# The mixer's input projection as plain fp32 products of the weights as loaded

## The chip, the cores and the metric

The kernel runs on one core of a Trainium2 chip. The time is device microseconds of one launch; three runs of the kernel before took 1105.32, 1108.52 and 1110.19 us (median 1108.52). The profile is one more execution, of 1107.35 us.

## The reference

Two layers work on 256 tokens of width 1024. Each layer is a gated feed-forward net (FFN), a token mixer and a second FFN, and each of these three adds its result to x and normalises:

```
mod = (silu(c) @ ada_w[l] + ada_b[l]).reshape(B, 3, 3, 1, 1024)
h = layernorm(x) * (1 + scale) + shift                     # from mod, for each of the three
f = (silu(h @ w_gate) * (h @ w_up)) @ w_down               # the FFN, inner width 2816
z = h @ w_in                                               # the mixer: 1024 -> 2048
q, k, v, u_ssm, u_pool = split(z, 512, 512, 512, 256, 256)
y = concat(dilated_attention(q, k, v), s5(u_ssm), pooling(u_pool)) @ w_out
x = layernorm(2**0.5 * x + w * gate * result) * gain + bias    # w = 1/2 for an FFN, 1 for the mixer
```

All inputs and outputs are fp32. The change is in `z = h @ w_in`, which is done twice, once in each layer.

## The kernel before

The 256 tokens are two tiles of 128 (called token tile 0 and 1, `tt` in the code). Weights come in pieces of 128 x 1024 fp32 (512 KB), each with one DMA from SyncE (line 374), into 41 slots of SBUF that all large tiles share. A weight piece `raw` is split into two fp32r tiles: ScalarE copies it to `hi` (line 379), VectorE writes `lo = raw - hi` (line 380). The activations are split in the same way into the two halves of `HT` (lines 508 and 509, in `parts`). A product is then three matmuls with one pass each, hi by hi, lo by hi, hi by lo (lines 544 to 546 in `linear`, 556 and 561 in `project`).

The input projection is four groups of 512 columns, named B (the inputs of S5 and pooling), V, Q and K. Each group has four weight pieces and is computed for both token tiles: 8 steps of 128 rows for each, so 64 steps of three matmuls in a layer and 128 in the kernel. Results are `pB`, `pV`, `pQ`, `pK`.

The mixer then runs, for each token tile: transposes (`ptr`), the S5 recurrence (matmul `pbu`, rotations and scans `w` on VectorE and GpSimd, matmul `py`), attention scores (`psc`, added to the bias `lg`, line 975), softmax, transposes of the weights (`ppt`), the weighted sum (`po`), pooling (`pz`), a gate (`pg`) and the output projection (`dm`).

Between two parts stands a chain for each token tile: `y` from the products (line 522), sums and statistics, the new x (line 453), statistics again with a power on GpSimd (line 441), `z` (line 471), a transpose `pn` on TensorE, the modulated `h` on ScalarE (line 481), and its split into `HT`. Two FFN units of token tile 0 can run while token tile 1 is in its chain.

Nobody writes the order by hand. Each operation is recorded with an engine and a cost, and a planner (`Plan.order`) simulates all engines, the slots and the PSUM banks, and emits the operations by planned start. On every engine the emitted order is then fixed: an instruction that waits holds back all behind it.

Of the kernel before, what the change touches and what calls it, by code (L numbers as in the profile page):

```python
# [48 lines left out]
LAG = {"PE": 0.2, "DVE": 0.14, "ACT": 0.14, "Pool": 0.12, "SP": 0.0}  # L49
SAME = {"PE": 0.003, "DVE": 0.125, "ACT": 0.125, "Pool": 0.1, "SP": 0.0}  # L50
WAIT = {"DVE": 0.25, "ACT": 0.25, "Pool": 1.3}
BUFS = {"w": N_W, "th": 2, "a": 2, "aT": 2, "st": 3, "carry": 1, "a3": 1, "gu": 2, "t": 2, "d0": 1, "d1": 1, "d2": 1, "d3": 1}
FREELY = ("t",)
PSUM_KINDS = ("gu", "t", "d0", "d1", "d2", "d3")
# [210 lines left out]
class Build:  # L265
    def __init__(self, tc, io, pools):
        self.tc, self.nc, self.io, self.pools = tc, tc.nc, io, pools
        self.plan = Plan()
        self.items, self.next = [], 0
        self.ready, self.acc, self.bc = {}, {}, {}  # L270
        self.exd, self.turns = [], []


# [94 lines left out]
    def process(self):  # L368

        nc = self.nc  # L370
        x = self.items[self.next]
        self.next += 1
        t = self.slot("raw")
        self.load(lambda: nc.sync.dma_start(out=t[:], in_=self.src(x)), [], [t], 0.5)
        if x[0] == "ada" and x[3] == 0:
            self.start_sum(*x[1:3])
        if x[0] in ("gu", "wd", "win", "wout"):
            hi, lo = self.slot("hi", F32R), self.slot("lo", F32R)
            self.act(1024, lambda: nc.scalar.copy(out=hi[:], in_=t[:]), [t], [hi])  # L379
# [77 lines left out]
    def modulated(self, tt, l, sub):  # L457

        for h, pt in enumerate(self.normed(tt, ("t", "t"))):
            hs = self.slot("h") if h == 0 else hs  # L460
            for k in range(4 * h, 4 * h + 4):
                self.shifted(hs, pt, k, tt, l, sub)
            self.parts(lambda h=h, hs=hs: hs[:, h * 512:(h + 1) * 512].rearrange("p (k t) -> p k t", k=4), [(hs, 4 * h + b) for b in range(4)], 4 * h, 4, tt)
# [20 lines left out]
    def first(self):  # L484

        pts = [list(self.normed(tt, ("t", "t") if tt == 0 else ("d2", "d3"))) for tt in range(2)]
        hs = [self.slot("h") for _ in range(2)]
        for k in range(8):
            for tt in range(2):
                self.shifted(hs[tt], pts[tt][k // 4], k, tt, 0, 0)  # L490
                self.parts(lambda tt=tt, k=k: hs[tt][:, k * 128:(k + 1) * 128].unsqueeze(1), [(hs[tt], k)], k, 1, tt)
# [43 lines left out]
    def linear(self, out, tt, pieces):  # L535

        nc = self.nc
        for kt in range(8):
            hi, lo = self.need(pieces[kt // 2])

            def go(kt=kt, hi=hi, lo=lo):
                xh, xl = (self.HT[:, p, kt, tt * 128:(tt + 1) * 128] for p in range(2))
                c = slice(kt % 2 * 512, kt % 2 * 512 + 512)
                nc.tensor.matmul(out[:], xh, hi[:, c], start=kt == 0, stop=False)  # L544
                nc.tensor.matmul(out[:], xl, hi[:, c], start=False, stop=False)  # L545
                nc.tensor.matmul(out[:], xh, lo[:, c], start=False, stop=kt == 7)  # L546
# [43 lines left out]
    def unit(self, l, sub, f, tt, u, d):  # L590
        nc = self.nc
        ps = self.bank("gu")
        self.linear(ps, tt, [("gu", l, f, u, q) for q in range(4)])
        th = self.buf("th", [128, 256])
        a = self.buf("a", [128, 256])
        self.act(256, lambda: nc.scalar.activation(out=th[:], in_=ps[:, 0:256], func=AF.Silu), [ps], [th])  # L596
        self.dve(256, lambda: nc.vector.tensor_tensor(out=a[:], in0=th[:], in1=ps[:, 256:512], op=ALU.mult), [th, ps], [a])  # L597
        pt = self.bank(shape=(128, 2, 128), name="pa")
        self.pe(0.22, lambda: [nc.tensor.transpose(pt[:, b, :], a[:, b * 128:(b + 1) * 128], self.ident[:]) for b in range(2)], [a, self.ident], [pt])  # L599
        t = self.buf("aT", [128, 2, 2, 128], F32R)  # L600
        self.act(256, lambda: nc.scalar.copy(out=t[:, 0], in_=pt[:]), [pt], [(t, 0)])  # L601
        self.dve(256, lambda: nc.vector.tensor_tensor(out=t[:, 1], in0=pt[:], in1=t[:, 0].bitcast(F32), op=ALU.subtract), [pt, (t, 0)], [(t, 1)])  # L602

        def down():
            for kk in range(2):
                w = self.need(("wd", l, f, u, kk))
                self.project(d, lambda kk=kk: t[:, 0, kk, :], lambda kk=kk: t[:, 1, kk, :], [t], w, u == 0 and kk == 0, u == NU - 1 and kk == 1)
        return down


# [211 lines left out]
    def mixer(self, l):  # L822
# [164 lines left out]
        def attend(tt):  # L987
# [13 lines left out]
            def go():  # L1001
                for h in range(8):
                    for i in range(tt + 1):
# [1 line left out]
            self.pe(1.75 * (tt + 1), go, keys + [(place("v"), ("v", i)) for i in range(tt + 1)], [p])  # L1005
            self.dve(512, lambda: nc.vector.tensor_tensor(out=ya(), in0=p[:], in1=dn[:, 0, tt, :].unsqueeze(2).to_broadcast([128, 8, 64]), op=ALU.mult),
                     [p, (dn, (0, tt))], [(place("qf"), ("f", tt))])
            self.turned(lambda k: qf()[:, tt, k * 128:(k + 1) * 128], [(place("qf"), ("f", tt))], 4, 0, tt)

        def glu(tt):  # L1010

# [15 lines left out]
            for d in range(2):  # L1027
                o = l * 2 + d
                self.act(128, lambda d=d, o=o: nc.scalar.activation(out=z[:, d, :], in_=pg[:, d, :], func=AF.Tanh, scale=0.25, bias=self.hb[:, o:o + 1]),
                         [pg, self.hb], [z], 0.1)  # L1030
            self.dve(256, lambda: nc.vector.scalar_tensor_tensor(out=z[:], in0=z[:], scalar=1.0, in1=yv[:], op0=ALU.add, op1=ALU.mult), [z, yv], [z])
            kh, kl = [[(HT, (p, kt, tt)) for kt in (4, 5)] for p in range(2)]
            self.act(256, lambda: nc.scalar.activation(out=HT[:, 0, 4:6, c], in_=z[:], func=AF.Copy, scale=0.5), [z], kh)
            self.dve(256, lambda: nc.vector.scalar_tensor_tensor(out=HT[:, 1, 4:6, c], in0=z[:], scalar=0.5, in1=HT[:, 0, 4:6, c].bitcast(F32),
# [4 lines left out]
        def pooling(tt):  # L1039
# [27 lines left out]
            self.pe(0.429, lambda: [nc.tensor.matmul(pz[:, j, :], px()[:, j, :], zp[:, j, :], start=True, stop=True) for j in range(2)], [zp, place("pg")], [pz])  # L1067
            c = cols[tt]
            for j in range(2):
                o = O_PS + l * 2 + j  # L1070
                kh, kl = [[(HT, (p, 6 + j, tt))] for p in range(2)]
                self.act(128, lambda j=j, o=o: nc.scalar.activation(out=HT[:, 0, 6 + j, c], in_=pz[:, j, :], func=AF.Copy, scale=sm[:, o:o + 1]), [pz, sm], kh, 0.1)
                self.dve(128, lambda j=j, o=o: nc.vector.scalar_tensor_tensor(out=HT[:, 1, 6 + j, c], in0=pz[:, j, :], scalar=sm[:, o:o + 1],
                                                                              in1=HT[:, 0, 6 + j, c].bitcast(F32), op0=ALU.mult, op1=ALU.subtract),
                         [pz, sm] + kh, kl)

        def out(tt):
            d = [self.bank(f"d{2 * tt + h}", name=f"dm{tt}{h}") for h in range(2)]
# [122 lines left out]
```

## Time and profile before

| | |
|---|---|
| the three runs | 1105.32, 1108.52, 1110.19 us |
| the profiled execution | 1107.35 us, its span 1105.6 us |
| TensorE busy | 1026.4 us (93%), mean granted clock 0.975 |
| VectorE busy | 864.6 us (78%) |
| ScalarE busy | 501.0 us (45%) |
| GpSimd busy | 300.3 us (27%) |
| read from HBM | 258.00 MB, 240 GB/s over the span |

TensorE has the largest share, but a share over the whole span mixes FFNs and mixers. The rows further down are by stage: the mixer of layer 0 lies at about 238 to 366 us of the span, that of layer 1 at about 772 to 895 us.

### The profile page before, as it was taken

The page shows a single profiled execution, that of the slowest core. Times are in us where ns is not written, and L with a number is a line of the kernel's source. Part 1 is how long each engine was busy: PE and PEld are TensorE (multiplying, and loading weights), DVE is VectorE, ACT ScalarE, POOL GpSimd, SP SyncE. Part 2 cuts the span into 40 slices and gives each one's busy share as a digit, 9 for nine tenths or more (in the row PEclk, how much of TensorE's full clock was granted, in tenths as well). Part 3 has the DMA queues.
Part 4 walks back from the last instruction along what each step waited for, and adds up shares of the span by engine and source line. Part 5 has one row for each costly group of instructions (what it writes and reads, how often), then busy time and mean ns, then how long its engine had stood idle before and what let it go on. Part 6 is the DMA issues. An engine that isn't in the chain of part 4 may idle for free. (4 is left out here: it accounts for less than half of the span.)

```text
span 1105.6 us, 13448 instructions
## 1 busy us (share of the span) xinstructions
PE 1026.4 (93%) x4626; PEld 802.6 (73%) x4626; DVE 864.6 (78%) x1254; ACT 501.0 (45%) x799; POOL 300.3 (27%) x449
## 2 busy tenths in 40 slices
PE   4899999979989799999999999999997989999996
PEld 3578877657767577788876887778775767887885
DVE  7978877998899899845389988758987999755423
ACT  3764444253356635434274544415425665544400
POOL 2057758023751100088610000001485010000000
PEclk9899999998998899999999999999998999999998
DMA  9988889984635489946486998968563447765601
GB/s 357 408 340 298 298 300 340 341 307 166 192 115 172 175 309 351 321 131 222 170 299 217 382 342 300 315 207 286 184 220 131 153 171 261 257 204 161 199 3 38
DMA packets 73551, 266.49 MB, mean 241 GB/s; under 512 B 8307, under 2 KB 8443, under 8 KB 73484
## 3 DMA queue, kind: packets, MB, share of 16 engines
q1 hardware_dynamic: 68556, 248.15, 63.5%
q0 software_dynamic: 4928, 17.50, 4.6%
q8 instruction: 36, 0.59, 0.2%
q14 instruction: 31, 0.25, 0.1%
HBM read 258.00 MB, written 7.61 MB: 240 GB/s over the span
## 5 line engine op out<-in xcount | busy, mean ns | idle before, releaser
L379 ACT CAST hi<-raw 128x1024 fp32r<-128x1024 f32 x312 | 323.0, 1052 | 205.2 <-DMA raw<-in_gu_dram 92.6
L380 DVE TENSOR_TENSOR lo<-raw,hi 128x1024 fp32r<-128x1024 f32 x312 | 379.7, 1237 | 42.0 <-ACT hi L379 38.2
L544 PE MATMUL gu<-hi,HT 128*128 128x512 f32 x704 | 291.2, 414 | 10.2 <-ACT hi L379 5.6
L546 PE MATMUL gu<-lo,HT 128*128 128x512 f32 x704 | 281.4, 400 | 8.5 <-DVE lo L380 8.5
L545 PE MATMUL gu<-hi,HT 128*128 128x512 f32 x704 | 283.7, 403 | 0.7 <-DVE HT L509 0.7
L556 PE MATMUL d<-hi,aT 128*128 128x512 f32 x672 | 183.5, 394 | 1.9 <-ACT aT L601 1.7
L546 PEld LDWEIGHTS gu<-lo,HT 128*128 128x128 f32 x704 | 134.2, 191 | 46.6 <-DVE lo L380 14.5
L544 PEld LDWEIGHTS gu<-hi,HT 128*128 128x128 f32 x704 | 134.4, 191 | 42.6 <-ACT hi L379 7.9
L545 PEld LDWEIGHTS gu<-hi,HT 128*128 128x128 f32 x704 | 134.8, 192 | 29.7 <-DVE HT L509 1.6
L556 PEld LDWEIGHTS d<-hi,aT 128*128 128x128 f32 x672 | 125.1, 188 | 33.4 <-ACT aT L601 3.6
L441 POOL TENSOR_TENSOR st<-st,power 128x1 f32<-128x1 f32 x24 | 27.9, 1160 | 385.6 <-DVE st L440 385.6
L388 DVE CUSTOM_DVE_ANT_0 raw<-raw,row,sm 128x1024 f32<-128x1024 f32 x96 | 123.3, 1295 | 3.6 <-DMA raw<-in_at_dram 3.6
L597 DVE TENSOR_TENSOR a<-th,gu 128x256 f32<-128x256 f32 x88 | 36.8, 419 | 99.4 <-ACT th L596 99.2
L596 ACT ACTIVATE th<-gu 128x256 f32<-128x256 f32 x88 | 33.7, 383 | 177.1 <-PE gu L546 176.9
L556 PE MATMUL d<-lo,aT 128*128 128x512 f32 x336 | 104.7, 393 | 0.0
L556 PEld LDWEIGHTS d<-lo,aT 128*128 128x128 f32 x336 | 63.1, 188 | 13.9
L932 POOL TENSOR_TENSOR w<-w 128x256 f32<-128x256 f32 x57 | 53.0, 945 | 50.8 <-DVE w L929 27.7
L395 DVE SCALAR_TENSOR_TENSOR acc<-raw,cond,acc 128x1024 f32<-128x1024 f32 x48 | 63.1, 1315 | 1.3 <-DMA raw<-in_ada_dram 1.3
L602 DVE TENSOR_TENSOR aT<-pa,aT 128x256 fp32r<-128x256 f32 x88 | 37.1, 421 | 33.8 <-ACT aT L601 33.1
L601 ACT CAST aT<-pa 128x256 fp32r<-128x256 f32 x88 | 32.9, 373 | 56.8 <-PE pa L599 56.5
L481 ACT ACTIVATE h<-pn,mod 128x128 f32<-128x128 f32 x96 | 36.8, 466 | 44.8 <-PE pn L475 24.9
L828 POOL DMA_DIRECT2D ex<-exd x2 | 1.1, 561 | 166.2 <-DMA raw<-in_gb_dram 149.5
(206 smaller groups left out, 1219.7 us busy)
## 6 DMA issues: line engine op xcount, KB each, us to landing
raw<-in_gu_dram SPq DMA_DIRECT2D x176, 512.0 KB, 5.3
raw<-in_at_dram SPq DMA_DIRECT2D x96, 512.0 KB, 6.2
raw<-in_wd_dram SPq DMA_DIRECT2D x88, 512.0 KB, 5.6
raw<-in_ada_dram SPq DMA_DIRECT2D x48, 512.0 KB, 5.3
raw<-in_win_dram SPq DMA_DIRECT2D x32, 512.0 KB, 6.3
raw<-in_wout_dram SPq DMA_DIRECT2D x16, 512.0 KB, 4.2
raw<-in_gb_dram SPq DMA_DIRECT2D x12, 512.0 KB, 5.5
lg<-biasd POOLq DMA_DIRECT2D x6, 512.0 KB, 5.8
```

Of the source, the lines that this page charges most:

```text
L379: self.act(1024, lambda: nc.scalar.copy(out=hi[:], in_=t[:]), [t], [hi])
L380: self.dve(1024, lambda: nc.vector.tensor_tensor(out=lo[:], in0=t[:], in1=hi[:].bitcast(F32), op=ALU.subtract), [t, hi], [lo])
L388: self.dve(1090, lambda: nc.vector.tensor_tensor_reduce(out=t[:], in0=t[:], in1=self.row[:], scale=1.0, scalar=self.sm[:, O_ADA + k:O_ADA ...
L395: self.dve(1090, lambda: nc.vector.scalar_tensor_tensor(out=acc[:], in0=t[:], scalar=self.cond[:, q:q + 1], in1=acc[:], op0=ALU.mult, op1= ...
L481: self.act(128, lambda: self.nc.scalar.activation(out=hs[:, k * 128:(k + 1) * 128], in_=pt[:, k % 4, :], func=AF.Identity, scale=sc(), bia ...
L544: nc.tensor.matmul(out[:], xh, hi[:, c], start=kt == 0, stop=False)
L545: nc.tensor.matmul(out[:], xl, hi[:, c], start=False, stop=False)
L546: nc.tensor.matmul(out[:], xh, lo[:, c], start=False, stop=kt == 7)
L556: nc.tensor.matmul(d[h][:], a(), b[:, c[h]], start=start, stop=stop)
L597: self.dve(256, lambda: nc.vector.tensor_tensor(out=a[:], in0=th[:], in1=ps[:, 256:512], op=ALU.mult), [th, ps], [a])
L602: self.dve(256, lambda: nc.vector.tensor_tensor(out=t[:, 1], in0=pt[:], in1=t[:, 0].bitcast(F32), op=ALU.subtract), [pt, (t, 0)], [(t, 1)])
L932: self.either(256, lambda eng, r=r, op=op: eng.tensor_tensor(out=x()[:, :, r, :], in0=x()[:, :, r, :], in1=y()[:, :, r, :], op=op), [kx, k ...
```

## The change

The pieces of `w_in` are used as loaded. They are no longer split, and each step of the input projection is one matmul call of fp32 `h` with fp32 `raw`. For this the tile `h`, whose split parts were all that was used before, is kept until the last of the four groups is done. The planner gets a cost of 0.86 for the new step; it had 0.695 for the three matmuls.

```
+WHOLE = ("B", "V", "Q", "K")
+WHOLE_UNITS = ()
...
-        if x[0] in ("gu", "wd", "win", "wout"):
+        if whole(x):
+            self.ready[x] = t
+        elif x[0] in ("gu", "wd", "win", "wout"):
             hi, lo = self.slot("hi", F32R), self.slot("lo", F32R)
...
-            hs = self.slot("h") if h == 0 else hs
+            if h == 0:
+                hs = self.hs[tt] = self.slot("h")
...
         for kt in range(8):
+            if whole(pieces[kt // 2]):
+                w, hs = self.need(pieces[kt // 2]), self.hs[tt]
+                self.pe(0.86, lambda kt=kt, w=w, hs=hs: nc.tensor.matmul(
+                    out[:], hs[:, kt * 128:(kt + 1) * 128], w[:, kt % 2 * 512:kt % 2 * 512 + 512], start=kt == 0, stop=kt == 7), [w, (hs, kt)], [out])
+                continue
             hi, lo = self.need(pieces[kt // 2])
...
+def whole(x):
+
+    return x[0] == "win" and x[2] in WHOLE or x[0] == "wout" and "O" in WHOLE or x[0] in ("gu", "wd") and x[3] in WHOLE_UNITS
```

The diff also holds such branches for the output projection and for FFN units; with these settings `whole` is false there and their products stay as they were. The split of `h` into `HT` (`parts`) is still done ahead of the mixer, though nothing in the input projection reads it any more.

For 32 of the 312 pieces that are split (the column xcount of lines 379 and 380) the ScalarE copy and the VectorE subtraction go. The planner's new costs change the order from the end of layer 0's first FFN on; up to there every engine has the same order as before.

TensorE, at the start of layer 0's mixer (`d` is the FFN's last product, `pn` the transpose for token tile 0, `pB` the first group), before:

```order
L561 MATMUL d_1_398<-hi_1848,aT_2074 128x512 x2
L561 MATMUL d_1_398<-lo_1915,aT_2074 128x512
L475 MATMUL pn_2104<-ident,z_2092 128x128 x4
L475 MATMUL pn_2111<-ident,z_2092 128x128 x4
L561 MATMUL d_1_399<-hi_1848,aT_2074 128x512 x2
L561 MATMUL d_1_399<-lo_1915,aT_2074 128x512
L544 MATMUL pB_2134<-hi_1948,HT 128x512
L545 MATMUL pB_2134<-hi_1948,HT 128x512
L546 MATMUL pB_2134<-lo_2014,HT 128x512
```

The same place after the change:

```order
L576 MATMUL d_1_398<-hi_1848,aT_2061 128x512 x2
L576 MATMUL d_1_398<-lo_1915,aT_2061 128x512
L576 MATMUL d_1_399<-hi_1848,aT_2061 128x512 x2
L576 MATMUL d_1_399<-lo_1915,aT_2061 128x512
L480 MATMUL pn_2093<-ident,z_2088 128x128 x4
L480 MATMUL pn_2102<-ident,z_2088 128x128 x4
L547 MATMUL pB_2113<-raw_1937,h_2107 128x512 x2
L547 MATMUL pB_2113<-raw_1958,h_2107 128x512 x2
L547 MATMUL pB_2113<-raw_1982,h_2107 128x512 x2
L547 MATMUL pB_2113<-raw_1991,h_2107 128x512 x2
L547 MATMUL pV_2151<-raw_2037,h_2107 128x512
```

The group B now reads `raw` and `h` and no `lo`, and the FFN's last products come ahead of the transpose.

TensorE, where layer 0's scores of token tile 0 (`psc`) meet the end of the group K (`pK`), before:

```order
L969 MATMUL psc_2681<-k_2674,qT_2513 128x128
L969 MATMUL psc_2682<-k_2674,qT_2513 128x128
L950 MATMUL py_2361<-w_337_2500,ex_1877 32x128 x4
L544 MATMUL pK_2608<-hi_2449,HT 128x512
L545 MATMUL pK_2608<-hi_2449,HT 128x512
L546 MATMUL pK_2608<-lo_2635,HT 128x512
L914 MATMUL pbu_2719<-uu_2258,ex_1877 128x128 x4
L864 MATMUL ptr_2729<-ident,kt_2725 128x128 x4
```

The same place after the change:

```order
L993 MATMUL psc_2513<-k_2507,qT_2331 128x128
L993 MATMUL psc_2514<-k_2507,qT_2331 128x128
L547 MATMUL pK_2505<-raw_2167,h_2209 128x512
L547 MATMUL pK_2505<-raw_2185,h_2209 128x512 x2
L547 MATMUL pK_2505<-raw_2194,h_2209 128x512 x2
L547 MATMUL pK_2505<-raw_2221,h_2209 128x512 x2
L938 MATMUL pbu_2556<-uu_2164,ex_1877 128x128 x4
L1017 MATMUL ppt_2564<-ident,lg_2237 128x128 x4
```

Before, one step of K was left behind the scores; now seven of token tile 1's eight steps are.

TensorE, at the end of layer 0's mixer (`dm` is the output projection of token tile 1, `pn` the transpose that the next FFN needs of token tile 0, `gu` that FFN's first product), before:

```order
L561 MATMUL dm_7_3084<-hi_2829,HT 128x512 x2
L561 MATMUL dm_7_3084<-lo_3022,HT 128x512
L561 MATMUL dm_3_3085<-hi_2829,HT 128x512 x2
L561 MATMUL dm_3_3085<-lo_3022,HT 128x512
L475 MATMUL pn_3183<-ident,z_3180 128x128 x4
L475 MATMUL pn_3191<-ident,z_3180 128x128 x4
L544 MATMUL gu_3215<-hi_2993,HT 128x512
```

The same place after the change:

```order
L480 MATMUL pn_2973<-ident,z_2959 128x128 x4
L571 MATMUL dm_7_2885<-hi_2593,HT 128x512
L571 MATMUL dm_3_2886<-hi_2593,HT 128x512
L571 MATMUL dm_7_2885<-hi_2593,HT 128x512
L571 MATMUL dm_3_2886<-hi_2593,HT 128x512
L571 MATMUL dm_7_2885<-lo_2768,HT 128x512
L571 MATMUL dm_3_2886<-lo_2768,HT 128x512
L576 MATMUL dm_7_2885<-hi_2621,HT 128x512 x2
L576 MATMUL dm_7_2885<-lo_2779,HT 128x512
L576 MATMUL dm_3_2886<-hi_2621,HT 128x512 x2
L576 MATMUL dm_3_2886<-lo_2779,HT 128x512
L555 MATMUL gu_3012<-hi_2723,HT 128x512
```

The transpose for the next FFN now stands ahead of the last twelve matmuls of the output projection, not behind them.

## Rows read from the trace of the kernel before

**Rows 1.** The page, busy time and share of TensorE and VectorE

```profile
PE 1026.4 (93%) x4626; PEld 802.6 (73%) x4626; DVE 864.6 (78%) x1254; ACT 501.0 (45%) x799; POOL 300.3 (27%) x449
```

**Rows 2.** Busy by stretch: PE, PEld, DVE, ACT, POOL, then PEclk, DMA share, GB/s

```profile
50.00:225.00 175.00, 169.11 (x726) 131.55 (x726) 144.03 (x214) 80.89 (x110) 99.52 (x144) 1.00 0.89 318
237.80:312.80 75.00, 65.66 (x322) 50.77 (x321) 65.21 (x97) 28.49 (x48) 41.31 (x53) 0.93 0.54 183
312.80:366.30 53.50, 47.43 (x269) 37.58 (x268) 50.07 (x89) 32.26 (x71) 12.53 (x16) 0.94 0.48 156
366.30:386.70 20.40, 14.36 (x54) 10.49 (x55) 19.45 (x28) 14.30 (x28) 2.39 (x2) 0.83 0.47 164
772.30:837.40 65.10, 63.41 (x330) 48.19 (x329) 56.47 (x94) 24.41 (x40) 43.37 (x57) 1.00 0.59 203
837.40:895.00 57.60, 50.27 (x261) 38.09 (x259) 52.59 (x85) 33.71 (x73) 11.07 (x14) 0.91 0.44 147
895.00:910.80 15.80, 12.00 (x50) 8.97 (x50) 14.02 (x22) 10.94 (x21) 2.38 (x2) 0.89 0.47 171
```

**Rows 3.** TensorE's waits, 237.8 to 386.7 us: total, times, longest

```profile
PE pB L546 <- DVE lo L380: 6.8, 1, 6.8
PE psc L969 <- DVE lg L975: 5.5, 1, 5.5
PE gu L546 <- DVE lo L380: 2.5, 1, 2.5
PE gu L544 <- ACT HT L508: 2.0, 1, 2.0
PE pB L544 <- ACT HT L508: 1.3, 1, 1.3
```

**Rows 4.** TensorE's waits, 772.3 to 910.8 us

```profile
PE psc L969 <- DVE lg L975: 3.0, 1, 3.0
PE gu L544 <- ACT HT L508: 2.1, 1, 2.1
```

**Rows 5.** TensorE's timeline in layer 0: start, duration, instruction

```profile
256.07 0.40 PE L544 MATMUL pV<-hi,HT 128*128 128x512 f32 x1
...
258.64 0.40 PE L546 MATMUL pV<-lo,HT 128*128 128x512 f32 x1
```

**Rows 6.** TensorE's timeline around one pair of plain fp32 products

```profile
180.76 1.88 PE L413 MATMUL pbc<-acc,ones 128*128 128x512 f32 x4
182.07 0.80 PE L544 MATMUL gu<-hi,HT 128*128 128x512 f32 x1
182.71 0.39 PE L545 MATMUL gu<-hi,HT 128*128 128x512 f32 x1
```

**Rows 7.** Line 413's matmuls, ns min/median/max, first and last start

```profile
L413 PE MATMUL pbc<-acc,ones x24: 591/592/696, 180.8 to 1014.6; 128*128 128x512 f32 x24
```

**Rows 8.** The page, the split of a weight piece

```profile
L379 ACT CAST hi<-raw 128x1024 fp32r<-128x1024 f32 x312 | 323.0, 1052 | 205.2 <-DMA raw<-in_gu_dram 92.6
L380 DVE TENSOR_TENSOR lo<-raw,hi 128x1024 fp32r<-128x1024 f32 x312 | 379.7, 1237 | 42.0 <-ACT hi L379 38.2
```

**Rows 9.** Short stretches with a lower granted clock (columns as in group 2)

```profile
251.80:256.00 4.20, 4.20 (x15) 3.70 (x14) 3.70 (x5) 3.08 (x9) 0.00 (x0) 0.50 0.00 0
333.00:339.00 6.00, 6.00 (x35) 4.50 (x36) 5.97 (x10) 3.03 (x12) 1.57 (x2) 0.59 0.54 175
379.00:386.00 7.00, 6.26 (x20) 4.57 (x20) 7.00 (x10) 6.38 (x15) 0.00 (x0) 0.52 0.24 76
```

**Rows 10.** VectorE's timeline in layer 0, token tile 1's chain

```profile
248.68 1.22 DVE L380 TENSOR_TENSOR lo<-raw,hi 128x1024 fp32r<-128x1024 f32 x1
250.34 1.00 DVE L471 TENSOR_SCALAR z<-X,st 128x512 f32<-128x512 f32 x2 [0.45 <-POOL st L441]
```

**Rows 11.** VectorE's timeline, scores of token tile 0 and first of tile 1

```profile
311.41 1.28 DVE L975 TENSOR_TENSOR lg<-psc,lg 128x512 f32<-128x512 f32 x2
...
332.02 0.68 DVE L975 TENSOR_TENSOR lg<-psc,lg 128x512 f32<-128x512 f32 x1
```

More of the change, by code (lines that the diff above doesn't have):

```diff
@@ L269, in __init__ @@
         self.items, self.next = [], 0
-        self.ready, self.acc, self.bc = {}, {}, {}
+        self.ready, self.acc, self.bc, self.hs = {}, {}, {}, [None, None]
         self.exd, self.turns = [], []
@@ L487, in first @@
         hs = [self.slot("h") for _ in range(2)]
+        self.hs = list(hs)
         for k in range(8):
@@ L547, in linear, with whole_product @@
             self.pe(0.695, go, [hi, lo] + [(self.HT, (p, kt, tt)) for p in range(2)], [out])
+    def whole_product(self, d, x, key, w, first, last):
+        for h in range(2):
+            self.pe(0.86, lambda h=h: self.nc.tensor.matmul(d[h][:], x(), w[:, h * 512:(h + 1) * 512], start=first, stop=last), key + [w], [d[h]])
     def project(self, d, xh, xl, key, w, first, last):
@@ L599, in unit @@
         self.pe(0.22, lambda: [nc.tensor.transpose(pt[:, b, :], a[:, b * 128:(b + 1) * 128], self.ident[:]) for b in range(2)], [a, self.ident], [pt])
-        t = self.buf("aT", [128, 2, 2, 128], F32R)
-        self.act(256, lambda: nc.scalar.copy(out=t[:, 0], in_=pt[:]), [pt], [(t, 0)])
-        self.dve(256, lambda: nc.vector.tensor_tensor(out=t[:, 1], in0=pt[:], in1=t[:, 0].bitcast(F32), op=ALU.subtract), [pt, (t, 0)], [(t, 1)])
+        if whole(("wd", l, f, u, 0)):
+            t = self.buf("aT", [128, 2, 128])
+            self.act(256, lambda: nc.scalar.copy(out=t[:], in_=pt[:]), [pt], [t])
+        else:
+            t = self.buf("aT", [128, 2, 2, 128], F32R)
+            self.act(256, lambda: nc.scalar.copy(out=t[:, 0], in_=pt[:]), [pt], [(t, 0)])
+            self.dve(256, lambda: nc.vector.tensor_tensor(out=t[:, 1], in0=pt[:], in1=t[:, 0].bitcast(F32), op=ALU.subtract), [pt, (t, 0)], [(t, 1)])
         def down():
@@ L606, in down @@
                 w = self.need(("wd", l, f, u, kk))
-                self.project(d, lambda kk=kk: t[:, 0, kk, :], lambda kk=kk: t[:, 1, kk, :], [t], w, u == 0 and kk == 0, u == NU - 1 and kk == 1)
+                first, last = u == 0 and kk == 0, u == NU - 1 and kk == 1
+                if whole(("wd", l, f, u, kk)):
+                    self.whole_product(d, lambda kk=kk: t[:, kk, :], [t], w, first, last)
+                else:
+                    self.project(d, lambda kk=kk: t[:, 0, kk, :], lambda kk=kk: t[:, 1, kk, :], [t], w, first, last)
         return down
@@ L839, in place @@
             return made[name]
+        mix = lambda tt: made[f"o{tt}"][:].rearrange("p (k t) -> p k t", k=8)
         V = lambda: made["v"][:].rearrange("p (s c) -> p s c", s=2)
@@ L1007, in attend @@
                      [p, (dn, (0, tt))], [(place("qf"), ("f", tt))])
-            self.turned(lambda k: qf()[:, tt, k * 128:(k + 1) * 128], [(place("qf"), ("f", tt))], 4, 0, tt)
+            if whole(("wout", l, 0)):
+                turn(lambda: qf()[:, tt, :], [(place("qf"), ("f", tt))], [lambda: mix(tt)[:, 0:4, :]], [(place(f"o{tt}"), 0)])
+            else:
+                self.turned(lambda k: qf()[:, tt, k * 128:(k + 1) * 128], [(place("qf"), ("f", tt))], 4, 0, tt)
         def glu(tt):
@@ L1031, in glu @@
             self.dve(256, lambda: nc.vector.scalar_tensor_tensor(out=z[:], in0=z[:], scalar=1.0, in1=yv[:], op0=ALU.add, op1=ALU.mult), [z, yv], [z])
+            if whole(("wout", l, 4)):
+                self.act(256, lambda: nc.scalar.activation(out=mix(tt)[:, 4:6, :], in_=z[:], func=AF.Copy, scale=0.5), [z], [(place(f"o{tt}"), 1)])
+                return
             kh, kl = [[(HT, (p, kt, tt)) for kt in (4, 5)] for p in range(2)]
@@ L1069, in pooling @@
             for j in range(2):
-                o = O_PS + l * 2 + j
+                i = O_PS + l * 2 + j
+                if whole(("wout", l, 6)):
+                    self.act(128, lambda j=j, i=i: nc.scalar.activation(out=mix(tt)[:, 6 + j, :], in_=pz[:, j, :], func=AF.Copy, scale=sm[:, i:i + 1]),
+                             [pz, sm], [(place(f"o{tt}"), 2)], 0.1)
+                    continue
                 kh, kl = [[(HT, (p, 6 + j, tt))] for p in range(2)]
-                self.act(128, lambda j=j, o=o: nc.scalar.activation(out=HT[:, 0, 6 + j, c], in_=pz[:, j, :], func=AF.Copy, scale=sm[:, o:o + 1]), [pz, sm], kh, 0.1)
-                self.dve(128, lambda j=j, o=o: nc.vector.scalar_tensor_tensor(out=HT[:, 1, 6 + j, c], in0=pz[:, j, :], scalar=sm[:, o:o + 1],
+                self.act(128, lambda j=j, i=i: nc.scalar.activation(out=HT[:, 0, 6 + j, c], in_=pz[:, j, :], func=AF.Copy, scale=sm[:, i:i + 1]), [pz, sm], kh, 0.1)
+                self.dve(128, lambda j=j, i=i: nc.vector.scalar_tensor_tensor(out=HT[:, 1, 6 + j, c], in0=pz[:, j, :], scalar=sm[:, i:i + 1],
                                                                               in1=HT[:, 0, 6 + j, c].bitcast(F32), op0=ALU.mult, op1=ALU.subtract),
@@ L1079, in out @@
             for kt in WOUT:
+                if whole(("wout", l, kt)):
+                    w = self.need(("wout", l, kt))
+                    self.whole_product(d, lambda kt=kt: mix(tt)[:, kt, :], [(place(f"o{tt}"), 0 if kt < 4 else kt // 2 - 1)], w, kt == WOUT[0], kt == WOUT[-1])
+                    continue
                 xh, xl = (lambda i=i, kt=kt: HT[:, i, kt, cols[tt]] for i in range(2))
```

## The prediction

> **What bounds the kernel now.** I read the page's busy shares first. TensorE is busy 93% of the span and VectorE 78% [rows 1], so the mean says that TensorE is the bound. Then the table by stretch, which shows that this is a mean of two kinds of stage. In an FFN (50 to 225 us) TensorE is busy 169 of 175 us at full clock. In layer 0's mixer and the start of the FFN behind it, 237.8 to 386.7 us, it is busy 127.5 of 148.9 us and the granted clock is 0.93, 0.94 and 0.83. VectorE is busy 134.7 us there. In layer 1 the first 65 us have hardly a gap, and the rest, 837.4 to 910.8, has 62.3 busy us of 73.4 at 0.91 and 0.89 [rows 2]. So around the mixers both engines are near their limit and take turns in waiting. Third, TensorE's waits there: in layer 0 one for `lo` in group B (6.8 us), one at the scores (5.5), and two where the next FFN starts (2.5 and 2.0) [rows 3]. In layer 1 the wait in B is missing and that at the scores is 3.0 [rows 4]. What follows such a wait runs at the lower level, 1.2 GHz, for some us: 0.50 of full clock from 251.8 to 256.0, 0.59 from 333 to 339, 0.52 from 379 to 386 [rows 9]. The change adds TensorE work in the mixers and takes VectorE and ScalarE work out of them.
>
> **The new step.** Three fp32r matmuls start 0.234 us apart: twelve of them from 256.07 to 258.64, eleven spacings in 2.57 us [rows 5]. A step costs 0.70 us. The plain fp32 product of the same shape stands in the kernel at line 413: two products appear as four records lasting 1.88 us together [rows 6], each of 0.592 us [rows 7], so three spacings take 1.29 us, 0.43 each, and a product of two records costs 0.86. The matmul that follows checks this: its successor starts at 182.71; less its own 0.234, the four took 1.72 us, again 0.43 each. As bounds I take the recorded start of the following matmul, 182.07 (0.655 a product), and of the one behind it, 182.71 (0.975). For 128 steps the three values give -5.8, +20.5 and +35.2 us. I take **+20.5**, 10.2 in each layer, since both readings of the row give it; its mean rests on products with one and the same weight, and the new ones load new weights each time, which the 0.43 us of a record should cover, as the 0.234 of the short one does now.
>
> The Trainium skill has a rule that is harder on the change: in "FP8 and Floating Point Precision", section "TensorE Precision Notes", true fp32 takes four passes through the array. With 0.234 us a pass that would be 0.94 a step and +30.2 us in all. The row shows 0.86; if the rule held as it stands, the forecast below would be 9.7 us later.
>
> **What goes.** 32 ScalarE copies of 1.052 and 32 VectorE subtractions of 1.237 us [rows 8], 16 in each layer: 16.8 and 19.8 us a layer. They count only where TensorE waits behind them. By place, in layer 0:
>
> *Start of the mixer.* TensorE waits 1.3 us for `HT` and 6.8 for `lo` [rows 3]. The new step needs `h` and a landed `raw` alone. I leave 0.8 us for the first `h` behind the transpose: 7.3 us go. The six us at half clock behind the wait (to 256.0, [rows 9]) held 3.0 us of work at full clock, so 3.0 go too. What is late next is token tile 1's chain: its `z` is ready at 251.3, with a subtraction at 248.68 [rows 10] beside the GpSimd step. In the new order its transpose stands behind B and seven steps of V: 238 + 15 x 0.86 + 1.5 for the short matmuls between is 252.4. It is covered by about 1 us. Gain 10.3.
>
> *Scores.* The 5.5 us and the slow stretch behind them (0.59 of full clock over 6 us is 4.9 us at half, 2.5 lost) are 8.0. No subtraction stands in what VectorE does there: from the adds of token tile 0's scores at 311.41 to the first add of tile 1 at 332.02 are 20.6 us of S5 and softmax work [rows 11]. But the new order puts tile 0's scores in front of seven steps of K (6.0 us) and not of one (0.7). Relative to TensorE, VectorE starts these 20.6 us 5.3 us earlier, about the wait. I take 6 of the 8.0; bounds 0 and 8.0.
>
> *Start of the FFN.* From 366.3 to 386.7 TensorE idles 6.0 us and loses 3.1 to the clock (0.52 over 7 us, 6.3 of them busy). The transpose now ahead of the last output products takes away the waits of tile 0 (2.0, and 0.8 of smaller ones). Tile 1's chain stays, less one or two subtractions of 1.2 us; the FFN unit in front of it (24 and 12 matmuls of 0.234 us, 8.4 in all) and the 6.0 us of waits cover it now, so I leave 3.5 of the 9.1. Gain 5.6; bounds 0 and 9.1.
>
> Layer 0: 10.3 + 6 + 5.6 - 10.2 = 11.7 gained.
>
> *Layer 1* has no wait in B to lose. It idles 11.1 us from 837.4 to 910.8 and 1.7 before, and loses about 5.8 to the clock (0.09 x 50.3 + 0.11 x 12.0) [rows 2], 18.6 in all. Its new order has the same places as layer 0's, so I leave it the same rest: 3.5 at the FFN, 2 at the scores, 3 in small waits. Gain 10.1 against 10.2: nothing.
>
> In the mixer the DMA engines are half busy [rows 2], and a piece now holds one slot where it held two, so the loads can only come earlier. For new waits that no row shows (a fixed order that was planned on other durations) I add 2.5; bounds 0 and 10. **Sum**: 11.7 + 0 - 2.5 = 9 us less than the profiled 1107.35, 1098.3. The median of the runs lies 1.2 above that execution, so **1099**.
>
> **Rivals.**
>
> *The waits are not the splits'.* (slower) The waits at the scores and at the FFN are at the end of chains that hold no subtraction [rows 11]. If TensorE, held longer by K, does not arrive later but VectorE does too, because S5's matmuls `pbu` and `py` that VectorE needs stand in the same queue between 0.86 us steps, these waits stay, and layer 1 loses its 10.2 whole. Then only the 10.3 of B are gained: 20.5 - 10.3 = +10, **1118**. It decides if tile 1's first score add comes over 20 us behind the end of K. Against it: VectorE is the busier engine here and loses 19.8 us; for it: layer 1's first 65 us show TensorE already full, where each longer step counts.
>
> *The FFN behind can't start earlier.* (no change) Its weights must land and be split; in the FFN the DMA engines are 0.89 busy [rows 2]. If they give the time back, layer 0 keeps its start alone, about break-even there, and layer 1 loses a few us in the mixer that the FFN would have lost to loads anyway: -2, **1106**. Against it: half of the DMA time in both mixers is free.
>
> *Four passes.* By 0.94 us a step the time would be 1099 + 9.7, **1109**.
>
> *All waits go.* Both layers lose 30.0 + 18.6 us of waits and clock and pay 20.5: 28 less, 1079. A half of what I left standing would give **1089**.
>
> **How the numbers follow.** Forecast (1091 to 1103) 0.61; waits stay 0.13; FFN held 0.17; four passes 0.04; more than forecast 0.05. A measurement of this kernel tells about 0.5%, 5.5 us, from no change: faster is under 1103, slower over 1114. The first and last case are faster, 0.66; the FFN case and the four passes, with a little of the others, no change, 0.22; 0.12 slower. The range leaves out the far ends: from 1088, where half of the remaining waits go, to 1113, where the score and FFN waits stay in one layer only.
>
> **What would show it.** Two records of about 0.59 us for each step, 0.43 apart, and 256 of them. No wait of `pB` over 1 us in layer 0, and full clock at 250 us. The end of K about where it was, near 312.8 us: the longer steps have then used up the gain of the start. The wait of `psc` in layer 0 under 2 us. The next FFN's first product right behind the last `dm`, near 366.3 - 10.3 - 6 + 10.2 = 360 us, with no wait for `HT`. In layer 1 the stretch from the first `pB` to the last `dm` about as long as before. The forecast is wrong if a product costs more than 0.95 us, if a wait over 3 us stands at `psc` or in front of `gu` in both layers, or if the FFNs show new waits for DMA.

## The result and the profile after

The changed kernel takes **1092.61 us** (median of four runs, 1089.63 to 1095.82), the kernel before 1106.95 beside it: a ratio of 0.9879, with a 95% interval of 0.9852 to 0.9906. That is 14.3 us less; 1099 was forecast, with a range of 1088 to 1113. The two profiled executions lie further apart, 1107.35 and 1089.63 us (spans 1105.6 and 1087.8), 17.7 us. The account below is of these two.

Busy times on the page (what stood in [rows 1] and [rows 8]):

```profile
PE 1031.0 (95%) x4498; PEld 772.7 (71%) x4498; DVE 830.2 (76%) x1224; ACT 471.4 (43%) x767; POOL 290.9 (27%) x447
...
L384 DVE TENSOR_TENSOR lo<-raw,hi 128x1024 fp32r<-128x1024 f32 x280 | 343.0, 1241 | 46.0 <-ACT hi L383 44.1
L383 ACT CAST hi<-raw 128x1024 fp32r<-128x1024 f32 x280 | 290.0, 1050 | 170.3 <-DMA raw<-in_gu_dram 89.7
```

The 32 subtractions that went had taken 36.7 us (379.7 less 343.0), and VectorE's busy time fell by 34.4. TensorE is busy 4.6 us longer only, though the longer steps add some 22: in part because less of its work ran at half clock (the mean granted clock is 0.987, before 0.975). The groups of the same shape by line, and TensorE's timeline in group V (start, duration, instruction):

```profile
L547 PE MATMUL pB<-raw,h 128*128 128x512 f32 x64 | 29.4, 602 | 0.1
```
```profile
253.22 7.03 PE L547 MATMUL pV<-raw,h 128*128 128x512 f32 x16
260.18 1.04 PE L938 MATMUL pbu<-uu,ex 32*128 32x128 f32 x7
```

Four groups of 64 are the 256 records. Sixteen of them take the 6.96 us up to `pbu`, 0.435 each and **0.87 a step**; the sum had 0.86. A wait of 0.1 us is left in B, where 6.8 and 1.3 stood [rows 3].

The same stretches as in [rows 2] (layer 0's B to K, the rest of the mixer, the start of the FFN; then layer 1's; columns as there):

```profile
236.70:307.80 71.10, 71.05 (x249) 35.68 (x249) 54.24 (x95) 25.79 (x59) 34.31 (x50) 1.00 0.56 200
307.80:355.80 48.00, 47.22 (x286) 38.20 (x285) 43.34 (x77) 29.46 (x62) 13.50 (x16) 1.00 0.43 143
355.80:380.00 24.20, 19.96 (x83) 15.10 (x82) 21.89 (x31) 13.39 (x23) 2.85 (x2) 0.93 0.55 207
760.90:830.10 69.20, 69.20 (x248) 35.00 (x246) 53.78 (x94) 22.67 (x51) 34.36 (x49) 1.00 0.50 177
830.10:878.20 48.10, 47.32 (x286) 38.29 (x286) 44.36 (x78) 29.81 (x61) 12.19 (x15) 1.00 0.42 143
878.20:901.00 22.80, 20.26 (x83) 14.47 (x82) 20.52 (x29) 14.85 (x23) 2.86 (x2) 0.93 0.48 168
```

Both mixers are now TensorE from end to end: 0.8 us idle in 119 and 0.8 in 117, all at full clock, where 65.66 of 75 and 47.43 of 53.5 were busy at 0.93 and 0.94 [rows 2]. What is still lost in these stretches lies at the FFN's start. TensorE's waits from 236.7 to 380 us (total, times, longest):

```profile
PE d L571 <- DVE lo L384: 2.0, 1, 2.0
PE pa L614 <- DVE a L612: 1.5, 1, 1.5
PE pz L1097 <- ACT pt L1020: 0.8, 1, 0.8
PE d L571 <- ACT aT L620: 0.5, 1, 0.5
PE pn L480 <- DVE z L476: 0.3, 1, 0.3
```

`psc` and `gu` of [rows 3] are gone, and `pa` and `d` have come. The last view is VectorE's adds of the scores, tile 0 and the first of tile 1:

```profile
302.11 1.27 DVE L999 TENSOR_TENSOR lg<-psc,lg 128x512 f32<-128x512 f32 x2
...
322.96 0.66 DVE L999 TENSOR_TENSOR lg<-psc,lg 128x512 f32<-128x512 f32 x1
```

VectorE needs 20.85 us between them, as before (20.6, [rows 11]). It did not get faster there. TensorE comes to the second eight `psc` of tile 1, where it had waited, 22.1 us behind tile 0's first add and not 15.9. It had 6.2 us more to do meanwhile, and K's six further steps are about 5.3 of them.

By place, as TensorE's lead over the kernel before at the same product of an FFN, or at a mixer's last `dm`: it is 1.2 us ahead of layer 0's mixer, where the order is still the same, so that is not the change's. It is 10.3 at layer 0's last `dm` (355.95 and not 366.25), 14.6 from 390 us of the kernel before on, 15.7 from 416 on, 14.75 shortly before layer 1's mixer and 12.35 behind one wait there, 16.6 at layer 1's last `dm` (878.33 and not 894.94), and 17.8 at the end. So layer 0's mixer gave 9.1, the start of the FFN behind it 4.3, layer 1's mixer 4.3 and the FFN behind it 1.2. The second execution of the changed kernel (below) has 4.4 at the same FFN's start.

The wait that costs 2.4 us is new. It stands in the last FFN ahead of layer 1's mixer; VectorE and TensorE there:

```profile
754.41 1.28 DVE L399 SCALAR_TENSOR_TENSOR acc<-raw,cond,acc 128x1024 f32<-128x1024 f32 x1 [2.48 <-DMA raw<-in_ada_dram]
756.08 0.44 PE L614 MATMUL pa<-ident,a 128*128 128x128 f32 x2 [2.41 <-DVE a L612]
```

VectorE waits for a piece of `ada_w`; the sum over it (line 399) stands ahead of the FFN's `a` in VectorE's fixed order. The kernel before has no such wait. All six traces in which the whole input projection is unsplit with 41 slots have it, 2.4 to 4.5 us at `pa`; none of the others does. That the pieces of `w_in`, now loaded earlier, hold up those of `ada_w` is likely, but not shown.

### The profile page after: what moved, and what is told of

Its sections match the earlier page's. It is cut to its first block, busy times and chain, and to the rows that moved or that the text cites. A ratio compares the mean times of both kernels' runs of the same rounds, so it can differ in the third digit from the quotient of the medians.

```text
span 1087.8 us, 13102 instructions
## 1 busy us (share of the span) xinstructions
PE 1031.0 (95%) x4498; PEld 772.7 (71%) x4498; DVE 830.2 (76%) x1224; ACT 471.4 (43%) x767; POOL 290.9 (27%) x447
## 4 chain that ended last, share of the span: by engine, by line
PE 49%; DVE 6%; DMA 6%; ACT 3%; issue 1%; POOLq 0%; DVEq 0%; SPq 0%; ACTq 0%
PE d L571 12%; PE gu L556 8%; PE gu L555 8%; PE gu L557 8%; DMA raw<-in_wd_dram 3%; DVE lo L384 3%; DMA raw<-in_gu_dram 2%; PE pa L614 1%; PE pQ L547 1%; PE pB L547 1%; PE pV L547 1%; PE pK L547 1%; DMA raw<-in_ada_dram 1%; ACT hi L383 1%; PE pbu L938 1%
## 5 line engine op out<-in xcount | busy, mean ns | idle before, releaser
L384 DVE TENSOR_TENSOR lo<-raw,hi 128x1024 fp32r<-128x1024 f32 x280 | 343.0, 1241 | 46.0 <-ACT hi L383 44.1
L383 ACT CAST hi<-raw 128x1024 fp32r<-128x1024 f32 x280 | 290.0, 1050 | 170.3 <-DMA raw<-in_gu_dram 89.7
L571 PE MATMUL d<-hi,aT 128*128 128x512 f32 x672 | 186.7, 398 | 2.0 <-ACT aT L620 1.9
L956 POOL TENSOR_TENSOR w<-w 128x256 f32<-128x256 f32 x55 | 46.4, 861 | 59.3 <-DVE w L953 33.2
L614 PE MATMUL pa<-ident,a 128*128 128x128 f32 x176 | 34.9, 280 | 17.4 <-DVE a L612 17.1
```

The lines of the kernel that those rows point to most:

```text
L571: nc.tensor.matmul(d[h][:], a(), b[:, c[h]], start=start, stop=stop)
L956: self.either(256, lambda eng, r=r, op=op: eng.tensor_tensor(out=x()[:, :, r, :], in0=x()[:, :, r, :], in1=y()[:, :, r, :], op=op), [kx, k ...
```

## The experiments

Five theories: **A**, VectorE's smaller load makes the gain; **B**, only the dependency does, the products no longer wait for `lo`; **C**, only the planner's new order; **D**, token tile 0's output products `dm` fill TensorE while VectorE works toward tile 1's scores, and this needs wout's splits early; **S**, they are early because the splits of `w_in` no longer hold slots. Ratios are to the kernel before on the same chip; its medians there were 1106.5, 1106.8 and 1105.9 us.

**The splits kept, unread.** The changed products, but the 32 pieces are still converted into slots of their own:

```
         if whole(x):
             self.ready[x] = t
+            hi, lo = self.slot("hi", F32R), self.slot("lo", F32R)
+            self.act(1024, ... copy(out=hi[:], in_=t[:]) ...)
+            self.dve(1024, ... tensor_tensor(out=lo[:], in0=t[:], in1=hi ..., op=ALU.subtract) ...)
```

> The changed kernel, but the 32 pieces of the input projection are still copied to hi on ScalarE and subtracted to lo on VectorE; nothing reads these two tiles, the products stay plain fp32. So the products no longer wait for a split, while the engines carry the old load (33.7 and 39.6 us). Theory A (the gain is the engines' relief): VectorE gets its 19.8 us in each mixer back, the waits at the scores return, and the time goes back to the kernel before or above it, ratio 1.00 to 1.02 (1107 to 1129 us). Theory B (the gain is that the products no longer wait for a split): the ratio stays near that of the change, 0.988 to 0.993 (1094 to 1099 us), and TensorE has no wait over 1 us in layer 0's group B.

Measured: 1113.4 us, 1.0075 [1.0046, 1.0105]. B falls: removing the dependency alone gains nothing, and the time is 0.5 to 1% above that of the kernel before. Its stretches 237 to 310 and 310 to 361 us, and its largest waits from 237 to 385:

```profile
237.00:310.00 73.00, 73.00 (x265) 37.32 (x262) 62.47 (x93) 27.36 (x49) 36.63 (x49) 1.00 0.55 187
310.00:361.00 51.00, 44.63 (x232) 34.55 (x231) 49.08 (x81) 29.83 (x67) 13.95 (x19) 0.80 0.41 136
```
```profile
PE py L977 <- POOL w L959: 4.2, 4, 2.0
PE gu L558 <- ACT HT L517: 2.0, 1, 2.0
```

To the end of K it is as good as the changed kernel. It loses everything behind that, at a clock of 0.80. At `psc`, where [rows 3] have 5.5, it waits 0.2 us only: seven steps of K stand behind tile 0's scores here too, and four `dm`. The run keeps the slots as well, so it does not part VectorE's time from them.

**The order alone.** The kernel before, with the planner told 0.86 for its old step (`self.pe(0.86 if pieces[0][0] == "win" else 0.695, ...)`).

> The kernel before with its three matmuls and its splits; only the planner's cost for a step of the input projection is 0.86, not 0.695, so the order is planned as for the longer step. Theory C (the new order alone gains): under 0.995 (below 1101 us). Theories A and B: no gain from the order, 0.997 to 1.010 (1104 to 1118 us), with the wait of pB for lo in layer 0 still there (about 6.8 us).

Measured: 1106.28 us, 0.9993 [0.9974, 1.0013]. C falls, as far as this order is the changed kernel's: seven steps of K stand behind tile 0's scores here too, and the wait of 5.5 at `psc` becomes two of 1.8. Group B still waits 5.3 us for `lo`, and nothing is gained in all.

**Without the unread split of `h`.** `parts` is skipped ahead of the mixer.

```
-            self.parts(...)
+            if not all(n in WHOLE for n in WIN) or sub != 1:
+              self.parts(...)
```

> The changed kernel without the split of h into HT ahead of the mixer, which nothing reads any more: in each layer 4 ScalarE copies (0.6 us) and 4 VectorE subtractions (0.69 us) go. If TensorE bounds the mixer now (my reading of the trace after): no gain beyond 1 us, ratio 0.986 to 0.990. If VectorE or ScalarE still bound it: 2 to 5 us less, ratio 0.983 to 0.986.

Measured: 1096.73 us, 0.9914 [0.9882, 0.9945]. It takes 5.6 us of VectorE's work away and gives nothing: less work on VectorE is not worth time where TensorE is full already. It says little of A elsewhere. The profiled execution is the slowest of six (1103.0); its wait for `ada_w` costs TensorE 4.5 us.

**The output projection too** (`WHOLE` with "O" added: wout's pieces are not split either).

> The changed kernel with the output projection too in plain fp32 products: 64 more pairs, each 4 records of 0.43 us for 6 matmuls of 0.234, +0.32 us each... in all 32 steps with two halves, 64 products, +0.16 us each, +10.2 us of TensorE; 16 more pieces are not split. If TensorE bounds the mixer now: 8 to 12 us slower than the change, ratio 0.995 to 1.000. If the splits' load on VectorE still counts there: gain again, under 0.988.

Measured: 1095.84 us, 0.9925 [0.9902, 0.9949], by ratio 4 to 5 us above the changed kernel. 64 more steps at +0.17 are 10.9 us. In the traces the mixers, from the FFN's last product to the last `dm`, grow by 3.8 us each, and the FFNs behind them shrink by 1.3 and 2.4; why was not followed.

**Group B alone** (`WHOLE = ("B",)`).

> Only group B's products (16 of the 64 steps' places in a layer, a quarter of the input projection) are plain fp32; V, Q and K stay split. TensorE work +5.1 us in all (32 steps by 0.16), VectorE 8 splits fewer (9.9 us in all, 4.9 a layer). Theory A (the gain is the wait in B plus VectorE's relief, about in proportion to the splits that go): the wait of pB for lo in layer 0 is gone (-6.8 and 3.0 of slow clock), TensorE pays 5.1, the second half keeps its waits at psc, py or gu for the most part: 1102 to 1106, ratio 0.993 to 0.998. Theory B (a dependency only, the place in B is all that counts): the whole of the 14 us gain, ratio 0.985 to 0.989. If every split counts the same: a quarter of the gain, 0.997.

Measured: 1099.95 us, 0.9943 [0.9918, 0.9967]. The wait in B is gone. The second halves keep theirs: in layer 0 `py` 4.0, `pn` 3.5 and `gu` 2.0, in layer 1 `dm` for `lo` 3.8 and `psc` 3.0.

**The output projection alone** (`WHOLE = ("O",)`). The input projection is as before.

> Here the output projection is plain fp32 and the input projection stays split: the same number of splits less (16 pieces a layer's 8 by two layers, half of the pieces of the input projection; 19.8 us of VectorE in both layers together counting the split of the mixer's output too), TensorE +10.2 us by 0.16 a step. Theory D (the gain in the second half of the mixer is that wout is ready early, so that token tile 0's output products fill TensorE while VectorE works on tile 1's scores): the wait in B stays (6.8), the waits at psc, py and gu shrink to under 2 us each, and the ratio is 0.993 to 1.002. If the second half gains by nothing but the end of K coming later: the waits stay and 10 us are added, ratio about 1.008.

Measured: **1089.21 us, 0.9836 [0.9807, 0.9864]**, faster than any theory said. Its largest waits from 236 to 390 us, and its stretches 310 to 361 and, from the last `dm` on, 368.7 to 393:

```profile
PE pB L557 <- DVE lo L384: 5.5, 1, 5.5
PE pB L555 <- ACT HT L514: 1.8, 1, 1.8
PE pa L614 <- ACT h L486: 1.2, 1, 1.2
```
```profile
310.00:361.00 51.00, 50.06 (x268) 32.73 (x267) 44.91 (x83) 30.82 (x72) 17.14 (x24) 1.00 0.38 125
368.70:393.00 24.30, 22.49 (x102) 17.70 (x101) 22.07 (x31) 10.87 (x21) 2.93 (x2) 1.00 0.49 171
```

The wait in B stands as before. The second half and the FFN's start are nearly full, at full clock, with half as many pieces freed as in the change. So what counts is which splits go. That the FFN's start would fill up too D had not said, and that is what lies beyond the expected range. D's reason is not what the trace shows at the scores: VectorE comes to tile 1's first add 14.1 us behind tile 0's (before 20.6), so the wait went because VectorE was early.

**ScalarE's table load earlier.** The changed kernel with a dummy Silu behind token tile 1's last tanh:

```
+            if tt == 1:
+                tb = self.buf("carry", [128, 16], name="tb")
+                self.act(8, ... activation(out=tb[:, 0:8], in_=z[:, 0, 0:8], func=AF.Silu) ...)
```

> The changed kernel with one tiny Silu activation on ScalarE behind the last tanh of token tile 1's mixer, so that ScalarE's table load (1.28 us) comes before the chain into the next FFN and not in front of that FFN's first Silu. Theory T (the wait of pa for a, 1.5 us in layer 0 and 1.9 in layer 1, is the table load): that wait falls under 0.5 us in both layers, the kernel is 1 to 3 us faster than the changed kernel on the same chip. Rival (it is the casts hi that wait for their DMA in front of it on ScalarE, or lo): the wait stays over 1 us and the time is the same within 1 us.

Measured: 1093.27 us, 0.987 [0.9842, 0.9899]. ScalarE around the new wait, in the changed kernel and then here (in brackets its own wait):

```profile
359.84 1.05 ACT L383 CAST hi<-raw 128x1024 fp32r<-128x1024 f32 x1 [0.29 <-DMA raw<-in_gu_dram]
360.91 1.28 ACT L611 ACT_TABLE_LOAD   x1
362.20 0.38 ACT L611 ACTIVATE th<-gu 128x256 f32<-128x256 f32 x1
```
```profile
361.87 1.05 ACT L383 CAST hi<-raw 128x1024 fp32r<-128x1024 f32 x1 [1.32 <-DMA raw<-in_wd_dram]
364.37 0.39 ACT L611 ACTIVATE th<-gu 128x256 f32<-128x256 f32 x1 [1.44 <-PE gu L557]
```

Theory T falls: the load went, and ScalarE then waited 1.44 us for the products themselves. The wait of `pa` fell from 1.5 to 1.1 us only, and in layer 1 from 1.9 to 0.9: the load was a part of it, and the time is the same as that of the next run within the noise.

**The changed kernel again**, beside the last three.

> The changed kernel once more, as it is, beside the others on one chip: ratio 0.985 to 0.991. Every theory expects the same; it gives the number against which the others of this call are set, and how far two measurements of one kernel lie apart.

Measured: 1093.95 us, 0.9889 [0.9859, 0.9919]; 1.3 us above the first measurement.

**wout's subtraction late.** The changed kernel; each `lo` of wout also reads the last maximum of tile 1's scores, so it can't come before that:

```
+        self.late = [(dn, (1, 1, 1))]
...
-  [t, hi], [lo])
+  [t, hi] + (self.late if x[0] == "wout" else []), [lo])
```

> The changed kernel, all loads, casts and slots as they are, but wout's subtraction lo may not run before the last maximum of token tile 1's scores, in both layers. VectorE does exactly the work of the changed kernel. Theory D (what the second half of the mixer gains is that wout is split ahead of those scores, so that token tile 0's output products dm fill TensorE behind them): dm can't run there, TensorE waits 6 us or more in each layer at py, pg, ppt or dm, and the kernel takes 1100 to 1110, ratio 0.994 to 1.003. Rival A (VectorE's smaller load alone, wherever it is taken away): no new waits over 2 us, the ratio stays 0.986 to 0.990.

Measured: **1109.19 us, 1.0029 [1.0011, 1.0047]**. VectorE does the same work (827.7 us in the profile, 830.2 in the changed kernel), and the whole gain is lost, 5.2 us of it in each mixer and the rest in the FFNs. So rival A falls: it matters when VectorE's work is done, and not only how much it is. From tile 0's first score add to tile 1's last, in the kernel before, the changed one and this one:

```profile
311.40:337.50 26.10, 20.37 (x122) 14.81 (x120) 25.97 (x55) 14.21 (x39) 11.74 (x16) 0.88 0.36 119
```
```profile
302.10:329.50 27.40, 27.40 (x151) 18.99 (x150) 26.48 (x52) 12.28 (x31) 12.72 (x15) 1.00 0.32 102
```
```profile
303.20:333.00 29.80, 24.48 (x140) 16.21 (x138) 26.04 (x54) 14.03 (x40) 11.51 (x14) 0.94 0.30 100
```

VectorE has 26 us of work there in all three (third busy figure). TensorE does 20.4, 27.4 and 24.5. TensorE's timeline here, and VectorE's adds of tile 0 and the first of tile 1:

```profile
321.22 1.13 PE L994 MATMUL psc<-k,qT 64*128 64x256 f32 x8
322.28 1.06 PE L975 MATMUL py<-w,ex 128*32 128x128 f32 x8
323.27 0.71 PE L1098 MATMUL pz<-zp,pg 128*128 128x128 f32 x4
328.91 1.95 PE L994 MATMUL psc<-k,qT 64*128 64x256 f32 x8 [4.92 <-DVE lg L1000]
```
```profile
303.27 1.29 DVE L1000 TENSOR_TENSOR lg<-psc,lg 128x512 f32<-128x512 f32 x2 [1.05 <-PE psc L994]
...
328.17 0.68 DVE L1000 TENSOR_TENSOR lg<-psc,lg 128x512 f32<-128x512 f32 x1
```

The wait of [rows 3] is back, as long in layer 1, though seven steps of K stand behind tile 0's scores as in the changed kernel. But VectorE is late itself: 24.9 us lie between these adds, 20.85 in the changed kernel. The planner ordered its S5 work otherwise, and it stands idle for 3.6 us of them (there 0.9). TensorE comes to this `psc` 1.4 us sooner than in the changed kernel, VectorE's add 4.1 later. In the changed kernel the same place reads:

```profile
321.83 0.38 PE L993 MATMUL psc<-k,qT 64*128 64x256 f32 x2
322.14 1.20 PE L571 MATMUL dm<-hi,HT 128*128 128x512 f32 x4
323.19 0.62 PE L571 MATMUL dm<-lo,HT 128*128 128x512 f32 x2
323.65 0.63 PE L571 MATMUL dm<-hi,HT 128*128 128x512 f32 x2
324.20 1.13 PE L993 MATMUL psc<-k,qT 64*128 64x256 f32 x8
```

From 316.27 to 332.68 the changed kernel runs 36 `dm`, 9.0 us (1.49, 2.06, 2.99 and 2.44 between the starts). Fourteen of them stand ahead of the second eight `psc` of tile 1, where the kernel before has ten and this run four; 22 stand behind those and ahead of the next `ppt`, where both others have none. So the gain needs wout's splits early. That the `dm` are what covers the wait at `psc`, as D has it, the run does not show.

**Fewer slots** (`N_W` 35 in place of 41; otherwise the changed kernel).

> The changed kernel with 35 slots in place of 41, VectorE's work unchanged. Theory S (the subtractions' disappearance gives slots back, wout's loads are issued at 259 to 291 us and not at 286 to 308, and this is what brings wout's splits ahead of the scores): with fewer slots the loads are issued late again, most of wout's splits come behind token tile 1's scores, TensorE waits 5 us or more in the mixers, 1098 to 1110, ratio 0.992 to 1.003. Rival (VectorE's time alone, slots don't matter): ratio 0.986 to 0.990. If the FFNs lose by fewer slots, it is seen in their stretches (50 to 225 us) and counted apart.

Measured: 1118.66 us, 1.0118 [1.0085, 1.0151]. Half an answer. SyncE's issues of wout's loads in layer 0, before, after, and here (the first of eight, then the other seven with the time they span):

```profile
285.57 0.33 SPq L374 DMA_DIRECT2D raw<-in_wout_dram  x1
291.36 17.04 SPq L374 DMA_DIRECT2D raw<-in_wout_dram  x7
```
```profile
258.57 0.33 SPq L376 DMA_DIRECT2D raw<-in_wout_dram  x1
264.31 27.06 SPq L376 DMA_DIRECT2D raw<-in_wout_dram  x7
```
```profile
279.13 0.33 SPq L376 DMA_DIRECT2D raw<-in_wout_dram  x1
285.54 29.78 SPq L376 DMA_DIRECT2D raw<-in_wout_dram  x7
```

TensorE's two largest waits within layer 0's mixer:

```profile
PE dm L571 <- DVE lo L384: 3.2, 1, 3.2
PE py L974 <- POOL w L956: 3.1, 2, 2.4
```

With fewer slots the loads are nearly as late as before, one `lo` alone stands between 280 and 337 us (six by 309 in the changed kernel), and layer 0's mixer is 5.9 us longer, 125.1 and not 119.2 from the first `pB` to the last `dm`. Layer 1's is 4.0 longer, 121.3 and not 117.3 from the FFN's last product to the last `dm`. That speaks for S. At `psc` there is no wait: VectorE's adds lie 21.3 us apart, and K's seven steps cover them with ten `dm`. The waits stand behind the scores, where the changed kernel runs 22 `dm` and this one two. So this is the place that early splits of wout fill. Most of the 25 us went elsewhere, in the FFNs and in a wait of 9.3 us in front of layer 0's mixer. How much of the early splits is due to slots, and how much to VectorE's time, stays open; the run that holds slots and leaves VectorE free was not made.

**B and the output projection** (`WHOLE = ("B", "O")`), and the same with B in layer 0 alone (`... and x[1] == 0`).

> Plain fp32 for group B and for the output projection, V, Q and K split. TensorE pays 5.1 + 10.2 us against the kernel before, 5.2 less than in the changed kernel. If the two places add up (the wait in B, -6.9 us alone, and the second half, -17.6 us alone): 1081 to 1085, ratio 0.977 to 0.980. If TensorE is then full: waits of under 2 us in the mixers and 1083 to 1089, 0.979 to 0.984. If only the order of the planner decides (order luck): 1089 to 1096, 0.985 to 0.990.

> As the one with B and the output projection, but B in plain fp32 in layer 0 only, since layer 1 has no wait in B. By the price of a step alone it is 2.5 us faster than that one (16 steps of 0.16 less); if VectorE's four splits in layer 1 are what makes room there, it is the same or slower by up to 3.

Measured: **1080.61 us, 0.9762 [0.9742, 0.9783]**, and 1083.24, 0.9774 [0.9752, 0.9796]. The intervals overlap, so the times do not tell the two apart. In the traces layer 1's mixer is 3.8 us shorter with its B whole, and layer 0's, set alike in both, 2.0 longer. The first beats the kernel before by 25 us and the changed one by 12 to 14: the two places add up (6.9 and 17.6 alone). Its busy times:

```profile
PE 1024.3 (95%) x4530; PEld 779.1 (72%) x4530; DVE 834.3 (77%) x1216; ACT 476.7 (44%) x775; POOL 297.0 (28%) x447
```

Against the run that also has V, Q and K whole it has 96 steps less in the long form. At 0.17 that is 16.3 us, and the medians differ by 15.2. But the price is not what the traces show: from the FFN's last product to the last `dm`, the mixers are 0.3 and 5.7 us shorter, the FFNs behind them 6.8 and 2.9. In layer 0 group V, split here, waits 1.6 us for `HT` and runs at a clock of 0.54 and 0.78 from 250 to 270 us; and the wait for `ada_w`, 4.0 us in the other run, is missing.

## Why the prediction was right, and where it was not

The direction held, and the time lies in the range. The gain was larger than forecast, mostly because two terms were too small: the first half of layer 0's mixer, and layer 1. Point by point:

- **The step**: 0.86 was taken, 0.87 measured, as two records of 0.435 us. No extra price came for loading new weights. The Trainium skill, "FP8 and Floating Point Precision", section "TensorE Precision Notes", has true fp32 take four passes through the array. The estimate of 0.94 that I made from it came out too high by 0.07; that speaks against the 0.234 us that I took for a pass, and not against the rule, since no run here shows how many passes a record holds.
- **Start of the mixer**: right in its mechanism. No wait in B, clock 1.00, tile 1's transpose covered. The size of the first half was too small: I had its gain of 10.3 used up by the price of 10.2, with K's end near 312.8. It ends at 307.8, and 75.0 us [rows 2] became 71.1, as the clock of 0.93 and the small waits of the whole stretch went too.
- **Scores**: right, in size (6 of 8.0; all of it went) and in reason. I had VectorE start its 20.6 us earlier, relative to TensorE, by K's seven steps. TensorE comes to `psc` 6.2 us later, and K is about 5.3 of that. Two runs with the same seven steps and fewer `dm`, the splits kept and the fewer slots, wait 0.2 and 0.0 us there. What I left out lies behind the scores. I had counted a subtraction only where TensorE waits behind it; those of wout matter too, as they come earlier when those in front of them go, and without that TensorE waits 3.2 and 3.1 us there.
- **Layer 1**: mis-sized, 0 forecast, 5.5 us measured with the FFN behind it. I left 5 us of waits standing in its mixer; 0.8 are left, all at full clock.
- **Start of the FFN**: nearly right in size, 5.6 forecast for layer 0, 4.3 measured by 390 us and 5.4 by 416. `gu` follows `dm` at once, at 355.8 (360 forecast), with no wait for `HT`; but 7.3 us later its unit's chain waits: `pa` 1.5, `aT` 0.5, `lo` 2.0, `z` 0.3, 4.3 in all, where 6.0 us had been idle. The lost time became shorter, and more of the stretch ran at full clock (0.93, before 0.83). The casts held by DMA (0.7 and 0.3 us) are a part of the new waits, and the table load 0.4. With wout freed instead this place has 22.49 of 24.30 us busy.
- **New waits**, 2.5 forecast: the size was luck. No row stood behind it, and the wait that came, 2.4 us for a piece of `ada_w`, I had not thought of. It goes against "the loads can only come earlier", and it is one of the signs that I had named for a wrong forecast, a new wait for DMA in an FFN.

From the forecast's -9.2 to the -17.8 us of the two traces: -3.0 for layer 0's mixer (9.1 gained, and 6.1 forecast as start, scores and price), -1.2 that was there ahead of it, +1.3 for the FFN's start, -5.5 for layer 1, and -0.2 for the new waits and the rest of the FFNs. By the medians 14.3 us were gained, so a part of these terms is scatter between executions. The rival "the waits stay" did not happen. The run with the splits kept came near its time, at 1113, but with other waits. Of "the FFN behind can't start earlier" a part is true, since the casts wait for DMA there (1.0 us in layer 0).

## What to carry to other kernels

Where a preparation step (here the split of weights) shares an engine with a chain that TensorE waits for, ask what else of that engine moves forward when one step goes, which products could then fill a wait, and which loads now meet others. Price it by place: fp32 products cost TensorE 0.17 us a step more. That was worth paying for the weights that start a stage and for wout; with V, Q and K whole on top the kernel took 15 us longer by the medians, in part in the mixers and in part in the FFNs.

## What the runs showed of the hardware

A ScalarE table load takes 1.28 us and stands in the engine's order; taking it out of the chain gave no time that could be measured. Over the 119 us of layer 0's mixer the granted clock was 1.00, in the 71 us that are mostly plain fp32 steps as in the 48 behind them.
